# RMSNorm and QKV projection on one core: whole row tiles stored at once, crossbar transposes in fours, and a new order of the head

## The chip, the cores and the metric

One core of one Trainium2 chip. The metric is the device time in microseconds of one execution. The profile is of one execution, taken by the hardware profiler.

## What is computed

`x` has shape (8, 1024, 768), `w_qkv` (768, 2304), all float32. The rows of `x` are normalized and multiplied by the matrix:

```python
rms = np.sqrt(np.mean(x ** 2, axis=-1, keepdims=True) + eps)
x_norm = x / rms * gamma
return np.matmul(x_norm, w_qkv).astype(np.float32)
```

Flattened, that is 8192 rows by 768, times 768 by 2304: 25.2 MB read, 7.1 MB of matrix, 75.5 MB written.

## The kernel before

**Tiles.** The rows make 64 row tiles of 128. The contraction of 768 makes six blocks `ko` of 128. Row tiles 0 to 3 are done **directly**: `mm` multiplies one block by 512 (or 256) columns of the bf16 matrix `w_b`, and `evac` scales the sum out of PSUM. All others go in **pairs** p = 2 to 31 (row tiles 2p and 2p + 1) by a Strassen-like scheme with seven products in place of eight, for each of three column chunks c of 768 columns. A product (`product`, L686) is three matmuls of 384 columns. `osum` makes the four sums s1 to s4 of a pair's blocks, `quad` and `tsum` the eight matrix blocks of a chunk. `hold` copies a partial result out of PSUM, `join` (VectorE) adds it to another, and `last` (ScalarE) writes the fourth quarter.

**Path of a row tile.** `load_x` (SP queue) brings 384 KB; `pstat` (ScalarE, L634) sums the squares, `prms` and `precip` make the factor, `pcast` (VectorE, L648) writes the scaled tile in f16. Then it is transposed: `pxbar` (L652) by a crossbar DMA from SP, or `ptr` and `pcp` (L671, L456 and L458) by six PE transposes and a copy. Before, row tiles 4, 5, 7 and 9 take the second way, the other 56 of the pairs the first. The first four tiles are cast to bf16 without the factor (`cast`), transposed by PE (`tr`, L480) and copied (`cp`); their statistics are `stat`.

**The matrix.** `load_w` brings it in 16 pieces, `conv(piece, ko, engine)` multiplies by gamma and writes `w_b`. `bound`, `fold`, `bound_tr`, `bound_top`, `bound_all` and `scales` find the f16 scale of a chunk.

**Output buffers.** A buffer of the pool `outp` holds 1024 columns of one row tile (12 buffers; four small ones of `outs` for columns 2048 on). `w_b` is free after the head, and pieces of it serve as output buffers too (`spare`, `lent`). `store` and `pstore` (L740) write a chunk of 768 or 1024 columns from SP as soon as it is whole: 384 KB in rows of 3072 B, mostly.

**Order.** Each engine works through its instructions in the order in which the program issues them, and that order is written out: `at(time, fn, ...)` puts a step into a list that is sorted by the time key. The keys of the head (`PLAN`, pairs 2 to 14) are literals and set an order; they are no measured times. From pair `STEADY` = 15 on a loop makes them, with z the key at which chunk c of pair p begins, one `SLOT` = 0.4875 us per product and 21 slots per pair:

```python
                    when((-96, -103)[odd] + 7 * i, load_x, t)
                    when((-64, -71)[odd] + 7 * i, pstat, t)
                    when((-41.2, -53.8)[odd] + 4.1 * i, pcast, t)
                    when((-38.2, -50.8)[odd] + 4.1 * i, pxbar, t)
```

SP's queue holds all loads of x and of the matrix, all crossbar transposes and nearly all stores, in one order.

**The start of the head.** SP loads x tiles 1, 0, 2, then matrix pieces 4, 1, 2, 3, x tile 3, pieces 0, 6, 7, 5. PE transposes gamma, runs 14 warming matmuls on zeros (`idle`, L555), then transposes tiles 1, 0 and 2, and begins the direct matmuls (L516). ScalarE runs cast, stat, three copies, two stats, and then conv(0, 0) (L450).

Of the kernel before, what the change touches and what calls it, by code (L numbers as in the profile page):

```python
# [15 lines left out]
HEAD_END = 166.25  # L16
# [3 lines left out]
    (0.000, "load_x", 1), (1.160, "load_x", 0), (1.580, "load_x", 2), (5.030, "cast", 0, "DVE"), (5.031, "load_w", 4),  # L20
    (5.032, "load_w", 1), (6.820, "cast", 2, "DVE"), (6.821, "cast", 1, "ACT"), (6.822, "stat", 0),
    (6.823, "load_w", 2), (6.824, "load_w", 3), (6.825, "gamma_in"), (6.826, "idle", 14, 512), (6.827, "tr", 1),
    (7.480, "conv", 4, 5, "DVE"), (7.481, "tr", 0), (7.482, "cp", 0, "ACT"), (7.483, "tr", 2),
    (7.484, "cp", 1, "ACT"), (8.050, "mm", 0, 0, "5"), (8.141, "conv", 1, 2, "DVE"), (8.266, "mm", 1, 0, "5"),
    (8.267, "load_x", 3), (8.801, "conv", 2, 3, "DVE"), (8.802, "cp", 2, "ACT"), (8.803, "mm", 0, 0, "2"),
    (8.926, "mm", 1, 0, "2"), (9.142, "mm", 2, 0, "5"), (9.371, "mm", 2, 0, "3"), (9.372, "stat", 1),
    (9.461, "conv", 3, 4, "DVE"), (9.587, "mm", 0, 0, "3"), (9.803, "mm", 1, 0, "3"), (10.031, "mm", 0, 0, "4"),
    (10.032, "recip", 0), (10.451, "stat", 3), (10.452, "load_w", 0), (11.772, "conv", 0, 1, "POOL"),
    (11.773, "mm", 2, 0, "4"), (11.774, "conv", 0, 0, "ACT"), (11.775, "cast", 3, "DVE"), (11.776, "mm", 1, 0, "4"),
    (11.777, "tr", 3), (12.612, "mm", 1, 0, "01"), (13.043, "mm", 0, 0, "01"), (13.044, "load_w", 6),  # L30
    (13.045, "load_w", 7), (13.046, "stat", 2), (13.047, "load_w", 5), (13.092, "conv", 6, 2, "POOL"),
    (13.093, "load_w", 10), (13.094, "cp", 3, "DVE"), (13.095, "bound", 0, 1, "DVE"), (13.831, "conv", 6, 3, "DVE"),
    (13.971, "bound", 0, 0, "ACT"), (14.261, "recip", 2), (14.262, "mm", 2, 0, "012"), (14.263, "mm", 3, 0, "012345"),
    (14.264, "load_w", 8), (14.361, "recip", 1), (15.571, "evac", 2, 0, "ACT"), (15.572, "recip", 3),
    (15.573, "load_w", 9), (17.054, "conv", 10, 5, "POOL"), (17.055, "mm", 0, 512, "23"),
    (17.056, "mm", 2, 512, "23"), (17.057, "conv", 7, 4, "DVE"), (17.058, "conv", 7, 5, "DVE"),
    (17.059, "mm", 1, 512, "45"), (17.060, "mm", 0, 512, "54"), (17.145, "mm", 3, 512, "45"),
    (17.146, "conv", 5, 1, "DVE"), (17.147, "evac", 3, 0, "ACT"), (17.576, "mm", 2, 512, "45"),
    (17.577, "load_w", 15), (17.578, "evac", 1, 0, "ACT"), (17.579, "conv", 5, 0, "DVE"),
    (18.008, "mm", 1, 512, "23"), (18.009, "bound", 1, 0, "ACT"), (18.010, "load_x", 5),  # L40
    (18.011, "bound", 0, 2, "DVE"), (18.554, "fold", 0), (18.555, "mm", 1, 512, "01"), (18.871, "bound_tr", 0),
    (18.872, "conv", 10, 4, "POOL"), (18.873, "evac", 0, 0, "DVE"), (18.971, "conv", 8, 0, "ACT"),
    (19.364, "bound_top", 0), (19.365, "load_x", 4), (19.366, "conv", 8, 1, "POOL"), (19.367, "mm", 3, 512, "01"),
    (19.695, "conv", 9, 3, "POOL"), (19.724, "bound_all", 0), (19.844, "mm", 2, 512, "01"), (20.044, "scales", 0),
    (20.045, "load_w", 14), (20.275, "mm", 1, 1024, "01"), (20.707, "mm", 3, 1024, "45"),
    (20.708, "evac", 1, 512, "ACT"), (21.139, "mm", 2, 1024, "01"), (21.140, "conv", 9, 2, "POOL"),
    (21.141, "evac", 2, 512, "ACT"), (21.142, "load_x", 7), (21.570, "mm", 0, 512, "01"),
    (22.002, "mm", 0, 1024, "23"), (22.003, "bound", 1, 2, "DVE"), (22.434, "mm", 3, 512, "23"),
    (22.435, "load_x", 6), (22.866, "mm", 2, 1024, "45"), (23.297, "mm", 3, 1024, "01"),
    (23.298, "quad", 0, "b22", "ACT"), (23.299, "quad", 0, "b12", "POOL"), (23.300, "bound", 1, 1, "DVE"),  # L50
    (23.301, "pstat", 5), (23.729, "mm", 3, 1024, "23"), (24.035, "fold", 1), (24.036, "pstat", 4),
    (24.037, "conv", 15, 3, "POOL"), (24.215, "conv", 15, 5, "ACT"), (24.216, "evac", 3, 512, "DVE"),
    (24.217, "mm", 0, 1024, "01"), (24.645, "prms", 2), (24.646, "bound_tr", 1), (24.845, "evac", 3, 1024, "DVE"),
    (24.846, "mm", 0, 1024, "45"), (24.895, "conv", 15, 4, "ACT"), (24.896, "load_w", 13), (24.897, "load_w", 12),
    (25.144, "mm", 1, 1024, "23"), (25.145, "quad", 0, "b11", "POOL"), (25.146, "load_w", 11),
    (25.325, "evac", 0, 512, "ACT"), (25.925, "evac", 0, 1024, "ACT"), (25.926, "mm", 0, 2048, "345"),
    (25.927, "mm", 1, 2048, "345"), (25.928, "bound_top", 1), (26.231, "bound_all", 1), (26.351, "mm", 1, 1024, "45"),
    (26.352, "conv", 14, 1, "POOL"), (26.353, "precip", 2), (26.354, "pcast", 5), (26.705, "conv", 14, 2, "DVE"),
    (26.965, "pcast", 4), (26.966, "pstat", 6), (26.967, "mm", 2, 1024, "23"), (26.968, "load_x", 15),
    (27.515, "tsum", 0, "t1", "DVE"), (27.516, "evac", 1, 1024, "ACT"), (27.517, "ptr", 5),  # L60
    (28.095, "conv", 13, 4, "ACT"), (28.215, "pcp", 5, "DVE"), (28.216, "conv", 14, 0, "POOL"),
    (28.217, "mm", 3, 2048, "345"), (28.218, "mm", 0, 2048, "012"), (28.735, "conv", 13, 5, "ACT"),
    (28.855, "osum", 2, "s1", "DVE"), (28.856, "mm", 3, 2048, "012"), (28.857, "mm", 2, 2048, "345"),
    (28.884, "ptr", 4), (29.244, "mm", 1, 2048, "012"), (29.572, "mm", 2, 2048, "012"),
    (29.573, "evac", 3, 2048, "DVE"), (29.574, "load_x", 12), (29.575, "pstat", 7),
    (29.818, "store", 3, 2, 2048, 256), (29.819, "scales", 1), (30.238, "load_x", 8), (30.239, "pcp", 4, "DVE"),
    (30.240, "quad", 0, "b21", "POOL"), (30.345, "evac", 0, 2048, "ACT"), (30.498, "evac", 1, 2048, "DVE"),
    (30.898, "evac", 2, 2048, "DVE"), (30.899, "mm", 1, 1536, "45"), (30.900, "conv", 12, 3, "POOL"),
    (31.038, "store", 1, 2, 2048, 256), (31.039, "conv", 12, 2, "POOL"), (31.040, "conv", 11, 0, "POOL"),
    (31.041, "quad", 1, "b21", "POOL"), (31.042, "mm", 3, 1536, "45"), (31.043, "mm", 3, 1536, "23"),  # L70
    (31.458, "store", 2, 2, 2048, 256), (31.459, "mm", 2, 1536, "23"), (31.460, "bound", 2, 1, "DVE"),
    (31.461, "conv", 11, 1, "ACT"), (31.462, "quad", 1, "b11", "ACT"), (31.626, "mm", 3, 1536, "01"),
    (32.575, "prms", 3), (32.576, "product", 2, 0, 1), (32.978, "evac", 2, 1024, "DVE"), (32.979, "product", 2, 0, 2),
    (33.033, "mm", 2, 1536, "45"), (33.034, "hold", 2, 0, "a", "p1", "ACT"), (33.638, "precip", 3),
    (33.639, "store", 0, 2, 2048, 256), (33.738, "join", 2, 0, 0, 0, "b", "p1"), (34.288, "pcast", 6),
    (34.289, "load_x", 17), (34.290, "load_x", 16), (34.291, "load_x", 11), (34.998, "osum", 2, "s2", "DVE"),
    (34.999, "mm", 0, 1536, "23"), (35.000, "mm", 1, 1536, "01"), (35.001, "mm", 2, 1536, "01"),
    (35.002, "bound", 2, 2, "ACT"), (35.003, "mm", 0, 1536, "01"), (35.191, "mm", 1, 1536, "23"),
    (35.192, "bound", 2, 0, "ACT"), (35.193, "quad", 1, "b22", "POOL"), (35.623, "product", 2, 0, 5),
    (35.624, "tsum", 0, "t2", "DVE"), (36.110, "mm", 0, 1536, "45"), (36.111, "pcast", 7),  # L80
    (36.568, "osum", 2, "s4", "DVE"), (36.569, "product", 2, 1, 1), (36.570, "pxbar", 6),
    (36.888, "osum", 2, "s3", "DVE"), (36.889, "evac", 1, 1536, "ACT"), (37.029, "product", 2, 1, 2),
    (37.030, "load_x", 23), (37.125, "hold", 2, 0, "c", "p5", "ACT"), (37.126, "quad", 1, "b12", "POOL"),
    (37.208, "tsum", 1, "t1", "DVE"), (37.517, "product", 2, 0, 6), (37.908, "tsum", 1, "t3", "DVE"),
# [275 lines left out]
CW = 384  # L360
# [8 lines left out]
def kernel(  # L369
# [8 lines left out]
    nc = tc.nc  # L378
    f32 = mybir.dt.float32
# [15 lines left out]
    MT = M // P  # L395
    NT = 512
    inv_k = 1.0 / float(K)
    PARTS = [(0, 1024), (1024, 1024), (2048, N - 2048)]

    singles = ctx.enter_context(tc.tile_pool(name="singles", bufs=1))  # L400
    wst = ctx.enter_context(tc.tile_pool(name="wst", bufs=12))
# [436 lines left out]
```

## Time and profile before

| | us |
|---|---|
| median of three runs | 354.19 (353.32 to 355.4) |
| the profiled execution, its own time | 353.78 |
| its span | 352.0 |
| PE busy | 341.8 |
| VectorE / ScalarE / POOL busy | 265.3 / 242.1 / 118.0 |
| first unbroken run of direct matmuls begins | 14.52 |
| PE ends; last work of the chain ends | 348.0; 348.9 |
| DMA moved | 119.19 MB, 339 GB/s in the mean |

The page gives busy time, share of the span and the count of instructions of each engine; the span in 40 slices of 8.8 us with the busy share in tenths; DMA queues; the chain of work that ended last; groups of instructions by source line; and DMA issues with the median time from issue to landing. PE busy 97% says little by itself: where PE has idle time, and what ended that, is read from busy time by stretches and from the chain. In a line of the stretches come the window, its length, then for PE, PE's weight loads, VectorE, ScalarE and POOL the busy time and the count, then PE's granted clock, the DMA share and GB/s.

### The profile page before, as it was taken

What the parts mean: (1) busy time and instruction counts of PE and PEld (TensorE: products, weight loads), DVE (VectorE), ACT (ScalarE), POOL (GpSimd) and SP (SyncE); (2) the same over time, 40 slices, a digit from 0 to 9 for tenths busy, and PEclk for the clock granted to TensorE, in tenths of its full rate; (3) what the DMA queues carried; (4) which work ended last, traced back from release to release, by engine and by line L of the source; (5) the groups of instructions that cost most, each with busy time, mean ns of one, the idle gap of its engine ahead of it and who ended that gap; (6) DMA issues with size and microseconds to landing.
All of it is one profiled execution on the core that took longest, in us unless ns stands there. A gap on an engine that the chain in (4) does not pass through costs nothing.

```text
span 352.0 us, 6558 instructions
## 1 busy us (share of the span) xinstructions
PE 341.8 (97%) x2079; PEld 201.4 (57%) x2082; DVE 265.3 (75%) x504; ACT 242.1 (69%) x497; POOL 118.0 (34%) x130
## 2 busy tenths in 40 slices
PE   6799999999999999999999999999999999999995
PEld 2346555666666666656666565656666666666663
DVE  2689989888788987786776859677686867767663
ACT  4999988966776756757758575766757677564543
POOL 0187237413123105244404444251614444163000
PEclk9999999999999999999999999999999999999999
DMA  7998999999999999999999999999999999998565
GB/s 267 391 383 295 311 405 309 331 313 374 314 301 374 338 411 340 371 384 314 359 374 316 404 341 365 346 386 354 356 344 326 369 327 373 314 380 301 202 260 223
DMA packets 86238, 119.19 MB, mean 339 GB/s; under 512 B 49206, under 2 KB 51132, under 8 KB 86204
## 3 DMA queue, kind: packets, MB, share of 16 engines
q1 hardware_dynamic: 86048, 118.68, 100.8%
q8 instruction: 16, 0.26, 0.3%
q14 instruction: 18, 0.15, 0.1%
q10 hardware_dynamic: 156, 0.10, 0.1%
HBM read 32.25 MB, written 75.50 MB: 306 GB/s over the span
## 4 chain that ended last, share of the span: by engine, by line
PE 92%; ACT 4%; DVE 1%; issue 1%; DMA 1%; DVEq 0%; ACTq 0%
PE pm L686 85%; PE pm L516 5%; PE pm L555 2%; ACT sq L576 1%; ACT xT L458 1%; DVE ot L711 1%; DMA g<-in_gamma_dram 1%; ACT ot L534 0%; ACT sq L467 0%; ACT pp L695 0%; PE pm L671 0%; DVE xb L648 0%; ACT w_b L450 0%; PE pm L480 0%; DVE pp L693 0%
## 5 line engine op out<-in xcount | busy, mean ns | idle before, releaser
L686 PE MATMUL pm<-wq,su 128*128 128x384 f16 x1080 | 203.8, 326 | 0.3 <-DVE pp L693 0.3
L695 ACT ACTIVATE pp<-pm,sc 128x384 f32<-128x384 f32 x207 | 116.5, 581 | 75.0 <-PE pm L686 72.7
L686 PE MATMUL pm<-wq,xT 128*128 128x384 f16 x807 | 159.3, 326 | 1.0 <-DVE ot L711 0.6
L686 PEld LDWEIGHTS <-su 128*128 128x128 f16 x1080 | 105.5, 98 | 70.1 <-issue 0.5
L711 DVE SCALAR_TENSOR_TENSOR ot<-pm,sc,pp 128x384 f32<-128x384 f32 x172 | 100.3, 611 | 23.6 <-PE pm L686 21.4
L686 PEld LDWEIGHTS <-xT 128*128 128x128 f16 x807 | 78.7, 98 | 54.1 <-issue 1.1
L666 POOL TENSOR_TENSOR su<-xT 128x384 f16<-128x384 f16 x52 | 49.6, 956 | 154.3 <-DMA xT<-xb 82.5
L711 DVE SCALAR_TENSOR_TENSOR w_b<-pm,sc,pp 128x384 f32<-128x384 f32 x98 | 58.1, 613 | 28.5 <-PE pm L686 24.5
L693 DVE TENSOR_SCALAR pp<-pm,sc 128x384 f32<-128x384 f32 x63 | 38.4, 614 | 19.1 <-PE pm L686 18.8
L634 ACT ACTIVATE sq<-x_t 128x768 bf16<-128x768 f32 x60 | 50.1, 835 | 2.1 <-DMA x_t<-in_x_dram 2.0
L648 DVE TENSOR_SCALAR xb<-x_t,rstd 128x768 f16<-128x768 f32 x60 | 41.0, 688 | 0.5
L715 ACT ACTIVATE ot<-pm,sc 128x384 f32<-128x384 f32 x48 | 27.5, 576 | 11.7 <-PE pm L686 11.7
L715 ACT ACTIVATE w_b<-pm,sc 128x384 f32<-128x384 f32 x41 | 23.4, 576 | 9.3 <-PE pm L686 9.3
L666 POOL TENSOR_TENSOR su<-su,xT 128x384 f16<-128x384 f16 x24 | 22.7, 948 | 19.6 <-DVE su L666 9.5
L516 PE MATMUL pm<-w_b,xT 128*128 128x512 bf16 (+1 forms) x117 | 25.1, 358 | 1.9 <-ACT w_b L450 0.9
L666 POOL TENSOR_TENSOR su<-xT,su 128x384 f16<-128x384 f16 x24 | 22.4, 933 | 8.7 <-DVE su L666 7.0
L516 PEld LDWEIGHTS <-xT 128*128 128x128 bf16 x120 | 11.2, 98 | 12.5 <-ACT xT L458 1.7
L452 POOL TENSOR_SCALAR w_b<-wq,g_sb 128x512 bf16<-128x512 f32 (+1 forms) x13 | 8.5, 665 | 18.0 <-DMA wq<-in_w_qkv_dram 18.0
L634 ACT ACTIVATION_READ_ACCUMULATOR sq<-x_t 128x1 f32 x60 | 11.5, 192 | 0.0
L618 POOL TENSOR_SCALAR wq<-w_b,inv 128x1152 f16<-128x1152 bf16 x8 | 10.1, 1266 | 3.2 <-issue 2.6
L638 ACT ACTIVATE rms<-ssq,eps_sb 128x2 f32<-128x2 f32 x30 | 8.8, 293 | 0.0
L573 DVE TENSOR_REDUCE bnd<-w_b 128x1 f32<-128x1536 bf16 x5 | 8.6, 1742 | 0.1
(57 smaller groups left out, 94.9 us busy)
## 6 DMA issues: line engine op xcount, KB each, us to landing
out_dram<-ot SPq DMA_DIRECT2D x110, 384.0 KB, 4.8
out_dram<-w_b SPq DMA_DIRECT2D x68, 384.0 KB, 5.0
x_t<-in_x_dram SPq DMA_DIRECT2D x64, 384.0 KB, 5.5
wq<-in_w_qkv_dram SPq DMA_DIRECT2D x10, 512.0 KB, 9.1
out_dram<-ot SPq DMA_DIRECT2D x8, 512.0 KB, 7.4
wq<-in_w_qkv_dram SPq DMA_DIRECT2D x4, 256.0 KB, 6.0
xT<-xb SPq DMA_TRANSPOSE x56, 5.0
wq<-in_w_qkv_dram SPq DMA_DIRECT2D x2, 384.0 KB, 9.5
```

What stands on the lines that cost most here:

```text
L516: nc.tensor.matmul(out=PM[t, n0][:, :nl], lhsT=XT[t][:, ko, :], rhs=w_b[:, ko, n0:n0 + nl], start=(b == 1), stop=(b == KO))
L573: nc.vector.tensor_reduce(out=o, in_=v, axis=mybir.AxisListType.XY, op=amax, apply_absolute_value=True)
L618: nc.gpsimd.tensor_scalar(out=o, in0=quad_view(c, q), scalar1=INV[c], scalar2=1.0, op0=mult, op1=mult)
L634: nc.scalar.activation(out=sq, in_=X[t], func=AF.Square, accum_out=SS[p][:, t % 2:t % 2 + 1])
L638: nc.scalar.activation(out=r, in_=SS[p], func=AF.Sqrt, scale=inv_k, bias=eps_sb)
L648: nc.vector.tensor_scalar(out=XB[t], in0=X[t], scalar1=SS[t // 2][:, t % 2:t % 2 + 1], scalar2=None, op0=mult)
L666: (nc.vector if eng == "DVE" else nc.gpsimd).tensor_tensor(out=block(p, q), in0=block(p, x), in1=block(p, y), op=op)
L686: nc.tensor.matmul(out=PB[k][:, :CW], lhsT=block(p, a)[:, ko, :], rhs=WQ[c, b][:, ko, :], start=(first and ko == 0), stop=(ko == KO // 2 - ...
L693: nc.vector.tensor_scalar(out=o, in0=pb, scalar1=SC[c], scalar2=None, op0=mult)
L695: nc.scalar.activation(out=o, in_=pb, func=AF.Copy, scale=SC[c], bias=0.0)
L711: nc.vector.scalar_tensor_tensor(out=result(p, c, i, j), in0=PB[p, c, bank][:, :CW], scalar=SC[c], in1=PART[p, c, held], op0=mult, op1=add)
L715: nc.scalar.activation(out=result(p, c, 1, 0), in_=PB[p, c, "a"][:, :CW], func=AF.Copy, scale=SC[c], bias=0.0)
```

## The change

**Output buffers** hold a whole row tile: `outp` has 5 buffers of 2304 columns, `outs` is gone, and three rows fit into `w_b` (row tiles t >= 8 with t % 8 in 1, 4, 6). A row tile is stored once, by `rstore`, when all its chunks are done: 1.18 MB in rows of 9216 B. Only the last pair is stored in parts. Where SP had about 195 stores it has 70.

**The steady loop** issues the four loads of two pairs in a row, the four transposes of two pairs in a row, and moves statistics and casts ahead by 21 slots, one pair. `xin` goes from 9 to 10 buffers, `xbp` from 4 to 6.

**The head** has a new order throughout. Row tiles 7 and 9 are transposed by the crossbar, not by PE; 6 warming matmuls are left of 14; SP loads x tiles 2 and 1, piece 4, tile 0, pieces 2 and 3, tile 3, pieces 0, 1, 6, 7, 5, 8, 10, 9; PE transposes tiles 2 and 1 ahead of the warming matmuls. Between the direct matmuls and pair 6 the key order on SP is: transposes of 6 and 7, load 12, store of row 3, load 10, row 2, load 14, row 0, transposes of 8 and 9, row 1, load 16, transposes of 11 and 10, load 15, row 4.

The diff, of `PLAN` only the first keys:

```diff
-HEAD_END = 166.25
+HEAD_END = 164.31
 STEADY = 15
 PLAN = [
-    (0.000, "load_x", 1), (1.160, "load_x", 0), (1.580, "load_x", 2), (5.030, "cast", 0, "DVE"), (5.031, "load_w", 4),
-    (5.032, "load_w", 1), (6.820, "cast", 2, "DVE"), (6.821, "cast", 1, "ACT"), (6.822, "stat", 0),
-    (6.823, "load_w", 2), (6.824, "load_w", 3), (6.825, "gamma_in"), (6.826, "idle", 14, 512), (6.827, "tr", 1),
...
+    (2.400, "gamma_in"), (2.401, "load_x", 2), (4.040, "stat", 2), (4.041, "load_x", 1), (5.240, "stat", 1),
+    (5.241, "load_w", 4), (5.242, "cast", 2, "DVE"), (5.243, "cast", 1, "DVE"), (5.244, "load_x", 0),
+    (5.245, "tr", 2), (5.670, "tr", 1), (6.030, "idle", 6, 512), (6.031, "load_w", 2), (6.490, "conv", 4, 5, "POOL"),
...
-    xin = ctx.enter_context(tc.tile_pool(name="xin", bufs=9))
+    xin = ctx.enter_context(tc.tile_pool(name="xin", bufs=10))
-    xbp = ctx.enter_context(tc.tile_pool(name="xbp", bufs=4))
+    xbp = ctx.enter_context(tc.tile_pool(name="xbp", bufs=6))
-    outp = ctx.enter_context(tc.tile_pool(name="outp", bufs=12))
-    outs = ctx.enter_context(tc.tile_pool(name="outs", bufs=4))
+    outp = ctx.enter_context(tc.tile_pool(name="outp", bufs=5))
...
+    spare = [N * i for i in range(KO // 2)]
+    lent = {}
+
+    def row(t):
+        if t not in OUT:
+            if t >= 8 and t % 8 in (1, 4, 6):
+                s = lent[t] = spare.pop(0)
+                OUT[t] = w_b.rearrange("p k n -> p (k n)").bitcast(f32)[:, s:s + N]
+            else:
+                OUT[t] = outp.tile([P, N], f32, name="ot")
+        return OUT[t]
...
+    def rstore(t):
+        nc.sync.dma_start(out=of[t * P:(t + 1) * P, :], in_=OUT[t])
+        if t in lent:
+            spare.append(lent.pop(t))
...
-                    when((-96, -103)[odd] + 7 * i, load_x, t)
-                    when((-64, -71)[odd] + 7 * i, pstat, t)
-                    when((-41.2, -53.8)[odd] + 4.1 * i, pcast, t)
-                    when((-38.2, -50.8)[odd] + 4.1 * i, pxbar, t)
-                when((-54.5, -61.5)[odd], prms, p)
-                when((-42, -54.6)[odd], precip, p)
+                    when((-96, -116.8)[odd] + 0.1 * i, load_x, t)
+                    when((-85, -92)[odd] + 7 * i, pstat, t)
+                    when((-62.2, -74.8)[odd] + 4.1 * i, pcast, t)
+                    when((-33.2, -54)[odd] + 0.1 * i, pxbar, t)
+                when((-75.5, -82.5)[odd], prms, p)
+                when((-63, -75.6)[odd], precip, p)
...
-                when(8.0, pstore, p, c, 0)
+                if final:
+                    when(8.0, pstore, p, c, 0)
+                elif c == N_CH - 1:
+                    when(8.0, rstore, 2 * p)
...
-                when(15.6, pstore, p, c, 1)
+                if final:
+                    when(15.6, pstore, p, c, 1)
+                elif c == N_CH - 1:
+                    when(15.6, rstore, 2 * p + 1)
```

## The prediction

> **What bounds the kernel now.** I read the busy line of the page first, then busy time by stretches, then the chain that ended last.
>
> ```profile
> PE 341.8 (97%) x2079; PEld 201.4 (57%) x2082; DVE 265.3 (75%) x504; ACT 242.1 (69%) x497; POOL 118.0 (34%) x130
> DMA  7998999999999999999999999999999999998565
> q1 hardware_dynamic: 86048, 118.68, 100.8%
> xT<-xb SPq DMA_TRANSPOSE x56, 5.0
> ```
>
> Two resources look full, TensorE and the 16 DMA engines. The stretches say which one sets the end.
>
> ```profile
> 8.48:14.50 6.02, 4.27 (x36) 2.37 (x35) 2.93 (x7) 5.09 (x11) 1.38 (x2) 1.00 1.04 394
> 30.00:42.00 12.00, 11.57 (x76) 6.78 (x76) 11.70 (x25) 11.23 (x20) 5.71 (x7) 1.00 0.89 261
> 220.00:260.00 40.00, 40.00 (x248) 24.06 (x246) 29.40 (x56) 27.45 (x59) 15.06 (x16) 1.00 1.07 361
> ```
>
> The first time after the stretch is its length, the next the PE time. From 220 us on PE never stops: 248 matmuls in 40 us, 163 ns each for 384 columns. DMA is full as well, but nobody on PE waits for it. So from there the change can only lose. From 14.5 us PE lacks some 0.4 us at 30 to 42, and 0.27, 0.22 and 0.42 us at 150, 195 and 217. The rest that can be won lies ahead of 14.52 us, in this chain (start, length, what):
>
> ```profile
> 3.06 5.58 PE pm L555 x14
> 8.64 0.69 PE pm L480 x12
> 9.35 2.20 ACT xT L458 x3
> 11.55 0.84 ACT sq L467 x2
> 12.71 0.83 ACT sq L467 x2
> 13.77 0.71 ACT w_b L450
> 14.52 0.59 PE pm L516 x2
> ```
>
> The 14 warming matmuls hold PE to 8.64, though VectorE and ScalarE had cast both first x tiles by 5.42. The transposes start late, so ACT's three copies do, so its statistics do, and the conversion conv(0,0) behind them ends at 14.5. PE waits 0.9 us for it. By 14.52 it has done 11 of 120 direct matmuls.
>
> **What the Trainium skill says.** *TensorE: Matmul & The Clock Gate*, Part 1: an idle array runs at half rate until about 3.4 us of sustained work. The trace agrees: warming matmuls start 0.425 us apart until 8.04 and direct ones 0.216 us apart later. It also says that ACT and DVE are strict first-in-first-out, so one late operand holds all that is queued behind it. *DMA: Bandwidth & Descriptors*, Anatomy of one DMA: a fixed 2.0 us plus bytes/436e3 (fitted on GpSimd's path). For a 1.18 MB row tile that makes an estimate of 4.7 us. The trace has no such transfer; its nearest row is the 384 KB store, 2.5 us near the end where DMA is free (the formula: 2.9) and 4.8 overall.
>
> **The change, part by part.** The sum is made against the profiled execution: 353.78 us, of which 352.0 is span. The median of the three runs is 354.19, 0.41 above it.
>
> *(1) Six warming matmuls instead of 14, behind two tiles' transposes: -1.1 us.* In the trace x tiles land at 3.87 and 4.86, and from the third on the conversions that wait for DMA (9.18 us at 1.97 MB queued, 12.36 at 3.15, 13.62 at 3.67) lie on a line of 0.38 MB per us. The new order queues x2, x1, w4, x0, w2, w3, x3, w0, w1, w6. So w0 (2.88 MB) lands at 11.6 instead of 12.4, and w1 (3.15 MB) at 12.3. Transposes of tiles 2 and 1 end by 6.1 on a cold array, the six matmuls at 8.7. Nine direct matmuls and two tiles' transposes follow; wholly cold they take 9 x 0.427 + 12 x 0.107 = 5.1 us, warm half of it; with the clock released near 10.5 they end by 12.3. The conversion of w1 on POOL (0.69) ends at 13.0, and 11 direct matmuls are done: where before stood at 14.52. That is 1.5 earlier. Against it, running closer to the loads costs about 0.25 (conv(6,2) now sits behind a stat and a bound on ACT, ready at 16.0, wanted at 15.76) and 0.2 (w10, landing at 19.1). Bounds: -1.9 (no feeding stall) and +0.5 (clock released a window later, and the loads lag 1 us).
>
> *(2) Tiles 7 and 9 go to the crossbar: -0.7 us, then +1.0.* Twelve PE transposes at 0.34 us for six are 0.68 us of PE time, all on the path, and the copies of 0.56 (DVE) and 0.81 (ACT) go. What replaces them is two DMAs on SP, 1.2 to 2.6 us to issue and 2.6 to 7.0 to land. Tile 9's comes behind tile 8's, some 6 us after its cast; VectorE's osum(4,s1) stands 3.7 us of work behind that cast and waits 1 to 2 us, with all joins behind it. The whole-row store of tile 1 is moved behind these two transposes on SP, and row 8 takes its buffer: VectorE's first join into it comes 6 to 7 us after the cast of 9, the store lands after 6 to 9. Both waits overlap; part is absorbed by PE's 8 PSUM banks. I take +1.0; bounds 0 and +2.5.
>
> *(3) The rest of the head: -0.3.* Three small gaps (0.27, 0.22, 0.42) had VectorE behind. The order there is new, so I take half of them as gone (-0.45), and +0.15 for ACT waiting on tile 15, whose load stands some 5.2 us ahead of its statistic (loads in steady state: 5.0 to 6.1). Bounds -0.9 and +1.5.
>
> *(4) 1.18 MB stores in place of 0.39 MB ones: 0.* About 190 stores become 70. SP's issue time is no bound: in two pairs' 20.5 us it issues 4 transposes (1.9 each, the median from 240 us on) and 8 copies (0.6), 12 us. The bytes stay, PE never reads a store. If this cover goes, it costs through buffers: 8 row buffers at 2 rows per 10.25 us are 41 us round, used for 8 us plus a landing of 5 to 8; some 25 us spare. Bounds 0 and +0.5.
>
> *(5) Transposes four in a row, casts and statistics one pair earlier: 0.* pstat, prms, precip and pcast all move by 21 slots, a whole pair, so ACT's and VectorE's order inside a pair is unchanged. Transposes still have 13 us to their first use against 5.0. With fewer changes between copies and transposes (one group in 20.5 us, not three; the rate falls to 134 GB/s at 243 us, behind such a group) DMA gains 1 to 2 us per two pairs, which nobody waits for.
>
> *(6) Loads four in a row, but 11 slots (5.4 us) ahead of the first statistic, not 32: 0, with a tail.* They are issued right behind the second row's store. Copies land one per 0.92 us when the queue is full, and 2.5 us after issue when it is empty: 1.6 + 2.75 for the row, + 0.92, gives 5.3 us after the store's issue. ACT wants the tile 6.0 us after it, and has about 0.3 us of slack. So 0 is likeliest; upper bound in the second rival.
>
> The tail (349 to 352) keeps its stores. Sum: -1.1 - 0.7 + 1.0 - 0.3 = -1.1, about 352.7 against 353.78, and **353.1** against the median.
>
> **The rivals.** *The head's gain stays whole.* If the landings of (2) come at 4 us and the small gaps go, it is -1.5 - 0.7 - 0.4 - 0.9 = -3.5 at most, 350.7 against the median. For it: VectorE lags only because PE did; PE idled 0.9 us just ahead of 14.52. Against it: from 20 to 60 us VectorE is 87 to 97% busy, and its work up to the cast of tile 8 is the same.
>
> *ACT starves in every second pair: slower.* The load behind the row's store lands late, ACT's pstat waits, the holds behind it wait, and PE cannot go on into a bank not read:
>
> ```profile
> 263.80 0.58 ACT L695 ACTIVATE pp<-pm,sc 128x384 f32<-128x384 f32 x1 [0.88 <-PE pm L686]
> 264.28 0.83 ACT L634 ACTIVATE sq<-x_t 128x768 bf16<-128x768 f32 x1
> 265.10 0.57 ACT L715 ACTIVATE ot<-pm,sc 128x384 f32<-128x384 f32 x1
> 265.57 0.58 ACT L695 ACTIVATE pp<-pm,sc 128x384 f32<-128x384 f32 x1
> ```
>
> The last of these must be read before a product 0.3 us later. If 1 us of transposes or of the earlier row's store is still queued when the row's store is issued, the tile lands 6.3 us or more after it, and anything past 6.3 is lost on PE, eight times (even pairs 16 to 30). At 0.5 us each that is 4 us: 357. It decides from 6.3 us. For it: DMA is full before. Against it: loads landed within 6.1 us of their own issue, behind as many bytes.
>
> *The store does what it says and nothing comes of it,* head included (the start's gain is eaten at pairs 4 and 5): 353.5 to 354.5. For it: the loads end the first waits in both orders.
>
> **How the numbers follow.** What can be told from no change here is 0.5%, 1.8 us. Small net gain or none (the sum and the last rival), from 352 to 355: 0.53, of it 0.13 below 352.4. Whole gain, 350.8 to 352.4: 0.22. Slower by ACT or by VectorE's waits, 355 to 359: 0.25. Faster is 0.13 + 0.22 = 0.35, same 0.40, slower 0.25. The range leaves out the lowest 5% and the highest 10%: 350.9 to 357.3.
>
> **What would show it.** Right: the first unbroken run of direct matmuls starts near 13.0, PE 100% busy from 220, PE matmul count down by 20, waits "DVE su <- DMA xT" and "DVE ot <- DMA out" of about 1 us near 55, transpose landings in one group. Wrong: "ACT sq L617 <- DMA x_t" or the like over 2 us in total, PE below 39.9 in 220 to 260, a start later than 14, or a product stream that is no earlier at 60 us.

## The result, and the profile after

The changed kernel takes **371.92 us** (median of four, 370.22 to 372.34) against 353.75 in the same comparison: a ratio of 1.0496, 95% interval 1.0447 to 1.0544. That is 18.2 us slower, where the prediction said 353.1 and at most 357.3. The profiled execution has a span of 370.2 us. Where one execution of a kernel lay over 1.5% above its fastest (one in all, 386.25 us in experiment 6), it is left out of the figures.

The busy line, the granted clock by slices, the queue and the loads of the page after (last number of an issue line: median us from issue to landing):

```profile
PE 344.5 (93%) x2059; PEld 201.8 (54%) x2062; DVE 273.1 (74%) x506; ACT 241.1 (65%) x495; POOL 121.5 (33%) x129
PEclk9999989999999989999999899999999999999999
q1 hardware_dynamic: 69792, 119.06, 95.1%
x_t<-in_x_dram SPq DMA_DIRECT2D x64, 384.0 KB, 6.9
```

PE does nearly the same number of matmuls (20 fewer, as foretold) in 18 us more. Bytes are nearly unchanged (119.06 MB on SP's queue against 118.68), and the queue is no fuller than before (95.1% against 100.8%). But loads of x land after 6.9 us in the median (5.5 before), and the clock row has three 8s, at 46 to 56, 130 to 139 and 204 to 213 us, where the row of the kernel before has only 9s.

Busy time by stretches, of after and, for the three with the largest loss, of before:

```profile
8.48:14.50 6.02, 4.97 (x32) 2.45 (x31) 4.06 (x13) 5.18 (x10) 0.69 (x1) 1.00 1.04 393
30.00:42.00 12.00, 11.72 (x69) 6.12 (x68) 10.93 (x20) 11.39 (x21) 7.38 (x8) 1.00 0.90 284
42.00:50.00 8.00, 5.88 (x28) 2.80 (x26) 7.44 (x13) 4.34 (x9) 4.35 (x3) 0.79 1.02 426
128.00:140.00 12.00, 8.63 (x44) 4.65 (x43) 5.56 (x11) 4.58 (x11) 4.25 (x5) 0.86 1.07 272
196.00:212.00 16.00, 11.50 (x62) 6.40 (x61) 7.78 (x15) 7.02 (x14) 2.18 (x3) 0.90 1.00 378
220.00:260.00 40.00, 39.47 (x243) 23.56 (x241) 30.78 (x54) 26.32 (x57) 15.60 (x15) 1.00 0.97 343
```

```profile
42.00:50.00 8.00, 8.00 (x50) 4.54 (x49) 6.42 (x16) 6.57 (x15) 4.51 (x4) 1.00 1.03 412
128.00:140.00 12.00, 12.00 (x76) 7.21 (x75) 9.23 (x18) 7.03 (x16) 4.42 (x5) 1.00 1.08 358
196.00:212.00 16.00, 15.78 (x98) 9.41 (x97) 11.04 (x21) 10.43 (x24) 5.13 (x6) 1.00 1.07 356
```

In stretches three to five of after PE does 28, 44 and 62 matmuls; before did 50, 76 and 98 there. At 0.163 us each the missing 22, 32 and 36 are 3.6, 5.2 and 5.9 us: 14.7 of the 18.2. The rest is smaller stops between 140 and 180 and a steady loss from 220 on (243 matmuls instead of 248 in 40 us). So the loss is not spread evenly: it sits in a few stops, and then a trickle.

What ends those stops (waits of after: who, for whom; total us, times, longest):

```profile
ACT sq L617 <- DMA x_t<-in_x_dram: 12.9, 5, 4.9
PE pm L669 <- ACT pp L678: 9.3, 4, 4.5
PE pm L669 <- DVE btop L573: 2.1, 1, 2.1
```

The first stop, at 42, ends on VectorE (the last line; see experiment 4). In the later ones ScalarE's pstat waits for its x tile, and PE waits for ScalarE's hold behind it. Three long waits of ScalarE, ended at 131.63, 157.51 and 206.68, are 12.1 of the 12.9 us. From 220 to 340 us it waits for x tiles only 0.2 us in all. The longest one, first on ScalarE and then on PE, from the timeline of after:

```profile
206.68 0.84 ACT L617 ACTIVATE sq<-x_t 128x768 bf16<-128x768 f32 x1 [4.88 <-DMA x_t<-in_x_dram]
207.43 0.19 ACT L617 ACTIVATION_READ_ACCUMULATOR sq<-x_t 128x1 f32 x1
207.53 0.56 ACT L689 ACTIVATE w_b<-pm,sc 128x384 f32<-128x384 f32 x1
207.99 0.57 ACT L678 ACTIVATE pp<-pm,sc 128x384 f32<-128x384 f32 x1
```

```profile
208.61 1.77 PE L669 MATMUL pm<-wq,su 128*128 128x384 f16 x6 [4.50 <-ACT pp L678]
210.18 2.12 PE L669 MATMUL pm<-wq,xT 128*128 128x384 f16 x6
```

After 4.50 us of idleness PE takes 1.77 and 2.12 us for six matmuls; six at 201.50, ahead of the stop, took 1.14. The granted clock in that time:

```profile
209.00:210.00 1.00, 1.00 (x5) 0.48 (x4) 0.21 (x1) 0.54 (x2) 0.00 (x0) 0.50 1.09 446
```

So the stop costs its length and some more, because PE starts again at half the clock (0.50): 5.9 us by the missing matmuls, for a wait of 4.50.

And why the load is late, in SP's queue of after around the burst at 140 us:

```profile
136.57 0.53 SPq L521 DMA_DIRECT2D out_dram<-ot  x1
137.19 1.49 SPq L521 DMA_DIRECT2D out_dram<-w_b  x1
138.74 1.18 SPq L521 DMA_DIRECT2D out_dram<-ot  x1
142.40 0.33 SPq L521 DMA_DIRECT2D out_dram<-w_b  x1
142.87 2.42 SPq L521 DMA_DIRECT2D out_dram<-ot  x2
145.34 5.15 SPq L418 DMA_DIRECT2D x_t<-in_x_dram  x4
```

Six row stores, 7.1 MB, are issued within 9 us (called the burst below), and the four loads right behind them. The tile view gives the loads' landings, the times from issue until the tile is there:

```profile
DMA to landing us min/median/max: 11.5/11.8/12.1
```

The plan has 5.4 us between the first of such four loads and its statistic; this distance is called the lead. The first two of the four are an odd pair's (in the loop `odd` is `(p + 1) % 2`, so the first number of `(-96, -116.8)[odd]` is for pairs 15, 17 to 31). The even pair's two have 24.8 slots, 12.1 us. The chain of waits runs through three loads of this kind:

```profile
123.03 8.59 DMA x_t<-in_x_dram
...
145.34 12.15 DMA x_t<-in_x_dram
...
196.36 10.30 DMA x_t<-in_x_dram
```

### The profile page after: what moved, and what is told of

The parts are those of the page before. It is cut to its first block, busy times and chain, and to the rows that moved or that the text cites. A ratio compares the mean times of both kernels' runs of the same rounds, so it can differ in the third digit from the quotient of the medians.

```text
span 370.2 us, 6171 instructions
## 1 busy us (share of the span) xinstructions
PE 344.5 (93%) x2059; PEld 201.8 (54%) x2062; DVE 273.1 (74%) x506; ACT 241.1 (65%) x495; POOL 121.5 (33%) x129
## 3 DMA queue, kind: packets, MB, share of 16 engines
q1 hardware_dynamic: 69792, 119.06, 95.1%
## 4 chain that ended last, share of the span: by engine, by line
PE 68%; DMA 18%; DVE 6%; issue 4%; ACT 2%; SPq 2%; DVEq 0%; ACTq 0%
PE pm L669 68%; DMA x_t<-in_x_dram 14%; DMA out_dram<-ot 2%; DMA wq<-in_w_qkv_dram 2%; DVE ot L685 1%; DVE xb L631 1%; DVE wq L607 1%; DVE w_b L685 1%; ACT pp L678 1%; SPq L521 1%; DVE pp L676 1%; SPq L418 0%; ACT sq L617 0%; SPq L423 0%; DVE su L649 0%
## 5 line engine op out<-in xcount | busy, mean ns | idle before, releaser
L669 PE MATMUL pm<-wq,su 128*128 128x384 f16 x1080 | 205.9, 329 | 9.3 <-ACT pp L678 9.3
L669 PE MATMUL pm<-wq,xT 128*128 128x384 f16 x807 | 161.2, 330 | 5.5 <-DVE btop L573 2.1
L685 DVE SCALAR_TENSOR_TENSOR ot<-pm,sc,pp 128x384 f32<-128x384 f32 x165 | 97.5, 612 | 48.4 <-PE pm L669 37.9
L649 POOL TENSOR_TENSOR su<-xT 128x384 f16<-128x384 f16 x49 | 48.1, 990 | 156.6 <-PE pm L669 92.8
L685 DVE SCALAR_TENSOR_TENSOR w_b<-pm,sc,pp 128x384 f32<-128x384 f32 x105 | 62.5, 611 | 15.8 <-PE pm L669 13.4
L617 ACT ACTIVATE sq<-x_t 128x768 bf16<-128x768 f32 x60 | 50.3, 838 | 13.2 <-DMA x_t<-in_x_dram 12.9
L689 ACT ACTIVATE ot<-pm,sc 128x384 f32<-128x384 f32 x68 | 38.8, 577 | 19.5 <-PE pm L669 19.4
L631 DVE TENSOR_SCALAR xb<-x_t,rstd 128x768 f16<-128x768 f32 x60 | 45.6, 765 | 0.4
L649 POOL TENSOR_TENSOR su<-su,xT 128x384 f16<-128x384 f16 x24 | 23.2, 966 | 28.6 <-PE pm L669 22.6
L649 POOL TENSOR_TENSOR su<-xT,su 128x384 f16<-128x384 f16 x27 | 26.6, 987 | 16.7 <-DVE su L649 8.6
L689 ACT ACTIVATE w_b<-pm,sc 128x384 f32<-128x384 f32 x21 | 12.1, 577 | 4.9 <-PE pm L669 4.8
L617 ACT ACTIVATION_READ_ACCUMULATOR sq<-x_t 128x1 f32 x60 | 11.6, 194 | 0.0
L431 ACT ACTIVATE w_b<-wq,g_sb 128x512 bf16<-128x512 f32 (+1 forms) x12 | 7.6, 644 | 2.2 <-DMA wq<-in_w_qkv_dram 2.1
```

The lines of the kernel that those rows point to most:

```text
L617: nc.scalar.activation(out=sq, in_=X[t], func=AF.Square, accum_out=SS[p][:, t % 2:t % 2 + 1])
L631: nc.vector.tensor_scalar(out=XB[t], in0=X[t], scalar1=SS[t // 2][:, t % 2:t % 2 + 1], scalar2=None, op0=mult)
L649: (nc.vector if eng == "DVE" else nc.gpsimd).tensor_tensor(out=block(p, q), in0=block(p, x), in1=block(p, y), op=op)
L669: nc.tensor.matmul(out=PB[k][:, :CW], lhsT=block(p, a)[:, ko, :], rhs=WQ[c, b][:, ko, :], start=(first and ko == 0), stop=(ko == KO // 2 - ...
L685: nc.vector.scalar_tensor_tensor(out=result(p, c, i, j), in0=PB[p, c, bank][:, :CW], scalar=SC[c], in1=PART[p, c, held], op0=mult, op1=add)
L689: nc.scalar.activation(out=result(p, c, 1, 0), in_=PB[p, c, "a"][:, :CW], func=AF.Copy, scale=SC[c], bias=0.0)
```

## The experiments

Names beginning with a_ are built on the kernel after, those with b_ on the kernel before. Ratios are against before, run beside each; in brackets the ratio and its 95% interval.

**1. Only the odd pairs' loads earlier: a part comes back.**

```diff
-                    when((-96, -116.8)[odd] + 0.1 * i, load_x, t)
+                    when((-117, -116.8)[odd] + 0.1 * i, load_x, t)
```

> The kernel after, and in its steady loop the two loads of an even pair 21 slots (10.2 us) earlier, so that loads go two and two instead of four in a row, each at least 25 slots ahead of its statistic. Theory 1 (the loads are too close to the statistics; ScalarE waits, PE stops and cools): the lost PE time at 128-140, 140-180 and 196-212 us (5.2, 3.1 and 6.2 us by the count of matmuls) goes nearly whole, the stop at 42-50 and the 2 us lost between 225 and 308 stay: 357 to 360. Theory 2 (the blocks on SP's queue, four transposes in a row behind 1.18 MB stores, delay whatever comes behind them; the loads are only the first to show it): the loads are still behind the same blocks, only a part comes back: 363 to 370.

By the code the pairs that this line moves are the odd ones, those with the lead of 5.4 us, and not the even ones.

Measured 363.68 us (1.0262, 1.022 to 1.0304): 8.2 us better than after, and at the lower end of theory 2's range. The stop at 128 to 140 is gone. Others came at 140 to 160, where VectorE waited for a row buffer whose store took 8.35 us to land, and at 220 to 260. The new place interleaves the loads with the transposes. The even pairs' loads, 12.1 us ahead, landed after 16.2 us at the burst (issued at 140.25) and after 11.4 us at 217.62.

**2. Only the transposes apart again: nothing.**

```diff
-                    when((-33.2, -54)[odd] + 0.1 * i, pxbar, t)
+                    when((-38.2, -50.8)[odd] + 4.1 * i, pxbar, t)
```

> The kernel after, and in its steady loop the transposes apart as in the kernel before (one every 4.1 slots, two groups per two pairs) instead of four in a row. Theory 1 (load lead): the loads keep their lead, and those at 123 us stand behind transposes of the head that are not moved, so 128-140 stays and the later stops get smaller only in part: 365 to 371. Theory 2 (blocks on SP's queue): SP is held 2 to 3 us at a time and not 7 to 10, the loads of the loop land within 7 us, the stops at 140-212 (9.3 us) go: 360 to 364.

Measured 370.9 (1.0469, 1.0411 to 1.0526). ScalarE waits 13.8 us for x tiles, not less. The 1.0 us to after is not clear of the noise. A block on SP made by the row of transposes is not the cause by itself.

**3. The loop's old slots under the new stores and the new head.** All six `when` lines of loads, statistics, factors, casts and transposes as before; `rstore`, buffers and `PLAN` as after.

> The kernel after with its whole-row buffers, row stores and head, but loads, statistics, casts and transposes of the steady loop at the slots of the kernel before. Theories 1 and 2 (timing of the loop): all stops from 128 us on go, the one at 42-50 stays: 355 to 358. Theory 3 (the 1.18 MB stores themselves burden the DMA queues or the buffers): the stores are all there, so 364 to 371.

Measured 357.12 (1.0082, 1.0059 to 1.0105). So 14.8 of the 18.2 us are the loop's slots, and 3.0 are the head and the row stores. What its tile view says of the same burst of stores (loads issued 139.4 to 148.9):

```profile
DMA to landing us min/median/max: 11.9/16.0/16.2
```

These loads are **slower** than those of after, and hardly anyone waits: 0.6 us of ScalarE in the whole run, because they have 15.6 us and more. The burst is there in both. But six lines changed, so this run alone doesn't tell the lead from the places of transposes, statistics and casts.

By count of matmuls the 3.0 us arise in two places. Up to 128 us PE did 706 against 735, up to 220 us 1254 against 1292; 20 of each difference are the warming matmuls and PE transposes left out by the change. So 9 are behind at 128 and 18 at 220, 1.5 and 2.9 us.

**4. One step of the head off POOL.** In the profile after, VectorE's osum at 41.52 takes 2.52 us and not 0.34, and ends as POOL's tsum does:

```profile
40.94 2.88 POOL L607 TENSOR_TENSOR wq<-wq 128x1152 f16<-128x1152 f16 x1
```

```profile
41.52 2.52 DVE L649 TENSOR_TENSOR su<-xT 128x384 f16<-128x384 f16 x1
```

```diff
-(45.841, "tsum", 1, "t4", "POOL")
+(45.841, "tsum", 1, "t4", "DVE")
```

> The kernel after with one step of the head, tsum(1, t4), on VectorE instead of POOL. In the profile VectorE's osum at 41.52 us takes 2.52 us instead of 0.34, until POOL's tsum (40.94 to 43.82) ends, and PE stops at 42.84. Theory A (VectorE was held off by POOL's instruction): the stop at 42-50 us (28 matmuls instead of 50, 3.6 us) gets smaller by 2 to 3.6 us: 368.3 to 370. Theory B (the stop has another cause, PE would wait for VectorE's queue anyway, which gets 0.74 us longer): 371 to 372.5.

Measured 372.49 (1.0502, 1.0453 to 1.0552): no gain, the time of theory B. Yet the same osum now took 0.35 us, and the stretch 42 to 50 did 44 matmuls instead of 28. VectorE had been held off beside POOL, as theory A says. Of the 16 matmuls gained, 2.6 us, 9 were left at 128 us, and at 220 the run was 3 behind after; ScalarE waited 15.6 us for x tiles in place of 12.9. A head that is ahead then waits longer for the next late tile.

**5. The old slots, but transposes in a row.**

```diff
-                    when((-38.2, -50.8)[odd] + 4.1 * i, pxbar, t)
+                    when((-27.5, -48.3)[odd] + 0.1 * i, pxbar, t)
```

> The kernel after with its row stores and head and the loop's slots of the kernel before (that was 357.1), but the four transposes of two pairs in a row (slots -27.5 and -48.3). Loads keep 32 slots of lead. Theory 1 (short lead of the loads): transposes in a row cost nothing by themselves, 356 to 358. Theory 2 (SP held by four transposes in a row behind 1.18 MB stores is a cause of its own, which is why only 8 of the 15 us came back with earlier loads): 360 to 366.

Measured 372.66 (1.0525, 1.0493 to 1.0557), worse than either theory said. Here the four transposes stand behind stores and loads, and SP's queue shows what that costs:

```profile
249.53 14.53 SPq L635 DMA_TRANSPOSE xT<-xb  x4
```

In after they stand behind two row stores only, and four take 6.5 us (276.12 to 282.65). A cycle of this kernel takes 23.2 us of SP (249.53 to 272.71) where PE needs 20.5. The edit also cut the transposes' lead to 10 us, against landings of 12.6 in the median from 225 to 300 us. So a row of transposes with that lead does harm, if it stands behind a backlog. Which of the two it is, the shorter lead or the row, this run doesn't tell.

**6. The old slots, but the loads late.**

```diff
-                    when((-96, -103)[odd] + 7 * i, load_x, t)
+                    when((-75, -95.8)[odd] + 0.1 * i, load_x, t)
```

> The same base (357.1), transposes apart, but the four loads in a row with the lead of the kernel after: 11 slots to the first statistic (slots -75 and -95.8). Theory 1: ScalarE waits for x tiles some 10 us in total and the stops come back: 364 to 371. Theory 2 (the short lead hurts only behind a row of transposes): 356 to 360.

Measured 379.64 (1.0714, 1.0667 to 1.0761): against number 3 the short lead of the loads, set in a row, costs 22.5 us, with transposes apart. That is worse than the whole change.

```profile
ACT sq L617 <- DMA x_t<-in_x_dram: 20.4, 8, 4.9
PE pm L669 <- ACT pp L678: 16.5, 8, 4.5
```

Eight waits for x tiles, eight stops of PE. From 120 to 330 us the loads landed after 5.4 to 8.3 us, 7.0 in the median; in after from 220 to 310 it was 5.7 to 6.9. These loads stand between two groups of transposes. That a lag in every cycle makes it worse than after fits this, but is not shown apart.

**7. The same line in the kernel before**, with its 384 KB stores.

> The kernel before with nothing changed but the loads of its loop: four in a row, 11 slots ahead of the first statistic instead of 32. Stores stay 384 KB, transposes apart. Theory 1 (lead alone): 362 to 370. Theory 3 (a late load also needs the 1.18 MB stores ahead of it in the queue): within 1 us of before's 354.2, up to 357.

Measured 363.75 (1.0259, 1.0222 to 1.0297): 9.6 us from one line, without any 1.18 MB store. ScalarE's waits in the whole run, and the landings of the loads from 120 to 330 us, where the lead was 5.4:

```profile
ACT sq L634 <- DMA x_t<-in_x_dram: 14.3, 9, 3.8
DMA to landing us min/median/max: 4.1/5.8/7.2
```

**8. Number 4 on the base of number 3.**

> The base of 357.1 us with tsum(1, t4) on VectorE instead of POOL. In the kernel after this step won 16 of the 22 matmuls lost at 42-50 us and gave all of it back at the later stops for x tiles. If those stops were the reason, they are gone here and the gain stays: 354 to 355. If the stop at 42-50 is slack of another kind (VectorE's 0.74 us more, later waits), 356.5 to 357.5.

Measured 356.67 (1.0069, 1.0041 to 1.0096): 0.4 us better, which is within the noise, and not 2 to 3. The stretch 42 to 50 has 43 matmuls instead of 28, but the chain of waits now runs through row buffers not yet stored, the first two of them new against number 3:

```profile
38.22 6.18 DMA out_dram<-ot
...
66.62 6.87 DMA out_dram<-ot
...
133.27 9.49 DMA out_dram<-w_b
```

A row buffer is free only after its last chunk and a landing of 6.2 to 9.5 us here. That this is what took the gain is read from the chain and not tested.

**9. Thirds from row buffers.** In the loop of after, `pstore` after each chunk in place of `rstore` after the third.

> The kernel after, but in its steady loop each row is stored in three parts of 384 KB, each as soon as its chunk is done, from the same whole-row buffers. Loads and transposes keep their slots. Theory 1 or 2 (lead of the loads, transposes in a row): it stays slow, 364 to 373. Theory 3 (1.18 MB stores issued together make the backlog that the loads stand behind): the stops from 128 us on go, 357 to 361.

Measured 378.62 (1.0688, 1.065 to 1.0725): 6.7 us slower than after. So the size of the loop's stores is not what makes it slow; large ones were a relief to it. The burst at 140 us is made of stores of the head and stays as it was.

**10. DMA alone,** the traffic of two pairs per cycle in five orders.

> DMA traffic alone, all on SP's queue, nothing computed (rows stored are zeros, the last part of each cycle is what is varied): per cycle the traffic of two pairs, 4 loads of 384 KB, 4 row stores of 1.18 MB, 4 transposes. Five orders: (1) copies, then four transposes in a row; (2) transposes two and two; (3) one transpose after each row and load; (4) no transposes; (5) as (1) with stores of 384 KB. The kernel after has 20.5 us per cycle. Theory 2 (a row of transposes does not overlap copies: 14.4 us of copies at 437 GB/s plus 6.5 us of transposes): (1) and (5) take 20.5 to 23 us, (4) 14 to 15.5, (2) and (3) less than (1) by 2 us or more. Rival (the grouping does not matter to DMA, only the place in the queue does): (1), (2), (3) within 1 us of each other.

Stretches of this kernel (length, then at the end the DMA share and GB/s; each one cycle, the third a mean over copies only; a single execution):

```profile
23.17:43.37 20.20, 0.00 (x0) 0.00 (x0) 1.00 1.04 351
89.49:107.63 18.14, 0.00 (x0) 0.00 (x0) 1.00 1.07 372
200.00:230.00 30.00, 0.00 (x0) 0.00 (x0) 1.00 1.03 421
276.30:296.94 20.64, 0.00 (x0) 0.00 (x0) 1.00 1.03 332
```

Four in a row: 20.2 us in each of three cycles. Two and two: 18.1, the next cycle 19.0. One after each row and load: 19.6 to 20.0. Without transposes 6.29 MB at 421 GB/s are 14.9. Thirds and four in a row: 20.6 and 21.6. Theory 2 had two and two about right and one at a time wrong. PE's cycle is 20.5 us. So the order of after leaves 0.3 us per cycle to make good a delay, thirds leave nothing, and two and two leave 1.5 to 2.4. The own order of the kernel before, with 384 KB stores and transposes apart, is not among the five. The DMA share is above 1.00 in all of them and tells none of this.

**11. Half the transposes away, the lead as in after.**

```diff
-                    when((-33.2, -54)[odd] + 0.1 * i, pxbar, t)
+                    when((-33.2, -54)[odd] + 0.1 * i, share if i else pxbar, t)
```

> The kernel after, but in its steady loop the odd row tile of each pair is not transposed: it uses the transposed tile of the even one (half of the rows hold wrong values from row tile 31 on). Everything else keeps its slot, the lead of the loads too; per two pairs two transposes, some 3.3 us of DMA, are gone. Capacity of DMA: with 3.6 us of slack in a cycle the lateness is made good, the stops from 140 us on go; the one at 128-140 can stay: 356 to 363. Lead alone: the loads still stand behind the rows' stores, 366 to 372.

Measured 367.31 (1.0373, 1.0345 to 1.0401), 4.6 us better than after, within the range of lead alone. ScalarE still waits 11.4 us for x tiles. Capacity is a part, not the whole.

**12. Loads from ScalarE's queue** (`nc.scalar.dma_start` in the loop).

> The kernel after with the loads of its steady loop issued from ScalarE's queue instead of SP's, at the same slots. SP's order (a load is issued only when SP is through with its transposes and stores): loads are issued on time and land within 7 us, the stops from 128 us on go at least by half: 357 to 364. Capacity of DMA or lead alone: the loads are issued earlier but share the same 16 engines with the rows' stores, landing 8 to 12 us: 366 to 375.

Measured 372.69 (1.053, 1.0497 to 1.0562). The loads landed no earlier, after 9.9 and 14.1 us in the first two groups and 8.5 us in the median of all. Yet ScalarE waited only 3.8 us for x tiles, not 12.9: in place of that it was held issuing four loads, 4.96 and 4.39 us in the first two groups, and PE waited behind it as before. So the run changes two things at once. It shows that another queue doesn't make the tiles land earlier; whether SP's order has a share in the loss it leaves open.

**13. How much lead?** In the kernel before, loads four in a row, the lead varied:

```diff
-                    when((-96, -103)[odd] + 7 * i, load_x, t)
+                    when((-96, -116.8)[odd] + 0.1 * i, load_x, t)      # b_row_loads
+                    when((-85.5, -106.3)[odd] + 0.1 * i, load_x, t)    # b_lead21
```

> The kernel before with the loads of its loop four in a row but 32 slots (15.6 us) or more ahead of the statistic. Lead alone: within 1 us of before, 353.5 to 355. Four in a row cost by themselves: 357 to 363.7.

> The same with 21.5 slots (10.5 us) ahead of the first statistic. If the lead has to cover the landing behind a backlog, and that is 5 to 8 us with 384 KB stores, it is enough: 353.5 to 356. If any shortening costs: near the middle of 354.1 and 363.8, 358 to 360.

Measured 354.38 (1.0021, 0.9997 to 1.0045) and 354.69 (1.0018, 1.0 to 1.0036). Four in a row cost nothing that can be told here. With 15.6 and 10.5 us of lead the time is that of before to 0.2%; with 5.4 it is 9.6 us more. Landings with 10.5 us, from 120 to 330 us:

```profile
DMA to landing us min/median/max: 5.3/6.6/8.5
```

The lead of 10.5 us is longer than the longest of these landings, the lead of 5.4 (number 7) shorter than the median of its own. Numbers 7 and 13 differ in this one line alone.

**14. And in the kernel after?** Loads behind the third row's store (9.2 us of lead), or ahead of the transposes (15.7 us):

```diff
-                    when((-96, -116.8)[odd] + 0.1 * i, load_x, t)
+                    when((-103.9, -124.7)[odd] + 0.1 * i, load_x, t)   # a_lead19
+                    when((-117.3, -138.1)[odd] + 0.1 * i, load_x, t)   # a_lead32
```

> The kernel after with its loads still four in a row, but right behind the third row's store of a cycle and not the fourth's: 19 slots (9.2 us) ahead of the first statistic instead of 11. Lead alone: the stops from 128 us on go by two thirds or more (landings of 12 us behind the burst at 140 still show), 358 to 363. If the row of transposes keeps it slow: 365 to 372.

> The kernel after with its loads ahead of the four transposes: 32 slots (15.7 us) of lead for the first statistic, but the transposes now stand behind two stores and four loads. Lead alone: all stops for x tiles go, the one at 42-50 stays: 356 to 359. If the row of transposes is late behind a backlog (12 to 15 us to land in the run with transposes in a row and long lead, against 13 us to first use here): 362 to 370.

Measured 367.15 (1.0363, 1.0333 to 1.0393) and 363.76 (1.0268, 1.0209 to 1.0326). Both lie in the range of the row of transposes. With 9.2 us the tiles behind the bursts are still late (landings up to 12.2 us). With 15.7 ScalarE waits for them only 0.6 us in all, and yet 6.6 us more are lost than in number 3. Waits of a_lead32:

```profile
DVE w_b L685 <- DMA out_dram<-w_b: 4.5, 1, 4.5
ACT sq L617 <- DMA x_t<-in_x_dram: 0.6, 1, 0.6
PE pm L669 <- DVE w_b L685: 5.3, 3, 4.0
```

What is late next is a row buffer: the store of an earlier row took 8.9 us, VectorE's join waited 4.5 for it, and PE did 89 matmuls from 140 to 160 us (122 before), 5.4 us. The chain of waits has a second late transfer, a transpose issued at 212.28 that took 7.00 us. By number 10 DMA has 0.3 us of slack per cycle with such a row of transposes. That whatever stands last in the queue is then late, x tiles in after, row buffers and a transpose here, fits all of this and is an inference.

**15. The first term of the prediction by itself,** in the kernel before:

```diff
-(6.826, "idle", 14, 512)
+(6.826, "idle", 6, 512)
```

> The kernel before with 6 warming matmuls instead of 14 and nothing else: the first term of the prediction by itself. If PE's late start is what delays the first direct matmuls, the unbroken run begins 0.5 to 1.2 us earlier than 14.52 us and the time is 0.3 to 1 us shorter. Rival: the loads of the matrix end the first waits in both, and the array is colder: within 0.3 us, or up to 0.5 us longer.

Measured **352.96** (0.9976, 0.9961 to 0.9991): 0.65 us faster than before beside it, clear of the noise though small. PE now waits for the load of matrix piece 0, from the chain of waits and the timeline:

```profile
4.64 8.41 DMA wq<-in_w_qkv_dram
```

```profile
13.91 6.42 PE L516 MATMUL pm<-w_b,xT 128*128 128x512 bf16 x28 [1.06 <-ACT w_b L450]
```

The unbroken run begins at 13.91 and not 14.52. Loading that piece earlier, ahead of x tile 3 (`load_x` 3 and its statistic and transposes moved behind):

> The kernel before with 6 warming matmuls (that was 353.0 against 353.6) and matrix piece 0 loaded ahead of x tile 3, tile 3's statistic and transposes behind the first use of piece 0. In the run with 6 warming matmuls PE waited 1.06 us for the conversion of piece 0, which waited for its load (issue 4.64, landing 13.05). If that load is the bound now, it lands 0.6 to 0.9 us earlier: 352.0 to 352.7. Rival: what is moved behind it (tile 3) is late instead: 352.8 to 353.6.

Measured 353.89 (0.9991, 0.9975 to 1.0006): what it brings is lost again. The first 15 direct matmuls then take 4.98 us, 0.33 each, where 11 took 2.73 with the 6 warming matmuls alone, 0.25 each. Whether the late tile 3 is the reason, as the rival says, is not shown.

## Why the prediction was wrong

**The step that failed is (6),** "Loads four in a row, but 11 slots (5.4 us) ahead of the first statistic, not 32: 0, with a tail". The mechanism was seen, and is the second rival: ScalarE starves, the holds behind pstat wait, PE cannot go on. Its terms were wrong in three places.
- *The landing.* The step counted 5.3 us from the store's issue to the tile, with one row store in the queue. In the steady part this came near: a store issued at 243.59, its tile there 6.2 us later, 0.07 us ahead of the statistic. At the stop of 206 us it was 10.7 (store issued 195.98, tile there at 206.66). The step has no term for the stretch between head and loop, where rows 8, 9 and 18 to 21 are stored together: six and five row stores stand ahead of the loads at 145 and 196 us, and two stores behind slow transposes ahead of those at 123. The argument against the rival, "loads landed within 6.1 us of their own issue, behind as many bytes", came from a queue fed with evenly spaced thirds, and from 240 to 300 us; over the whole loop of before, 120 to 296 us, they took up to 6.7, past the 6.3 from which the rival decides. Number 7 shows that even there 5.4 us would have been too short.
- *The price of a stop.* For "At 0.5 us each that is 4 us" came 9.3 us of PE in four waits, up to 4.5 each, and after two of them PE started again at half its clock (granted 0.50 from 134 to 137 and from 209 to 212 us). A small lateness in every cycle was priced; what came was large and in the transition. The rival also named the wrong pairs: the short lead is that of the odd pairs, nine of them from 15 to 31.
- *The chance.* 0.25 for slower, for a wait with 0.3 us of slack against a full queue, was too little. A margin cut from 15.6 to 5.4 us beside landings of 5.0 to 6.1 should have been the likeliest case.

**(5) was wrong in sign,** as far as number 10 goes. The step said that DMA gains 1 to 2 us per two pairs with fewer changes between copies and transposes. Number 10 measures a row of four as the slowest order with 1.18 MB stores: 1.2 to 2.1 us more than two and two, 0.2 to 0.6 more than one at a time, and 20.2 of PE's 20.5 us. Numbers 11 (4.6 us) and 14 (6.6 us still lost with the long lead) show that the transposes have a part in the loss. The trickle from 220 us on is not explained by the row alone: a_lead19, with the same row, did 248 matmuls from 220 to 260 as before did, though 289 against 298 from 260 to 308.

**(4), the stores: 0 was half right.** The estimate of 4.7 us for a 1.18 MB store met medians of 5.5 and 4.9 us (from `ot` and from `w_b`). The size costs DMA nothing, rather the reverse (numbers 9 and 10). But "8 row buffers, some 25 us spare" holds for evenly spaced rows only. Around the burst a buffer's store landed after 8.9 to 9.5 us (numbers 8 and 14). Once the x tiles were on time, PE waited 0.9 us behind it in number 8 and lost 5.4 us in number 14.

**(1) was right in mechanism,** and in the change itself larger than expected: at 14.5 us 20 direct matmuls are done where before had done 11, and the first unbroken run begins at 11.80, not near 13.0. By itself, without the new order of the loads, the shorter warming gave 0.65 us (number 15). PE was at full rate earlier than the 10.5 us of the step: seven direct matmuls from 8.92 on took 1.67 us, 0.24 each. Of the clock the prediction says that its trace agrees with "about 3.4 us of sustained work"; it agrees in the half rate, but the warming matmuls from 2.99 on kept to that rate until 8.04, 5.0 us.

**(2) and (3) gave the start away again.** At 40 us all direct matmuls are done in both kernels, and after is 8 products' matmuls ahead of before (26 against 18), 1.3 us; at 50 us it is 12 behind. Head and row stores together are +3.0 (number 3), where -1.1 was expected. The wait foreseen near 55 us ("DVE su <- DMA xT") did not come; the one that came, VectorE beside POOL's tsum at 41.5 us, 3.6 us of PE at 42 to 50 of which number 4 got 2.6 back for a time, was not on the list.

Three of the signs named for a wrong forecast are in the profile: 12.9 us of "ACT sq L617 <- DMA x_t", PE at 39.47 in 220 to 260, and a product stream that is no earlier at 60 us (121 matmuls of products against 131). The sign of a late start is not: the start was early.

**Shown and not shown.** Shown: on the base of before the lead decides by itself (5.4 against 10.5 us: 9 us), on the base of number 3 it does too (22.5 us); the loop's slots are 14.8 of the 18.2 us; smaller stores in the loop don't help. Shown as a part: the row of transposes. Not settled: how the 14.8 us divide between lead and transposes, since the two are not additive (8.2 come back with the loads moved ahead of the transposes, 1.0 with spread transposes, 14.8 with both and the old places of statistics and casts), and whether SP's order has a share.

## What to carry to other kernels

The lead of a prefetch (a load issued ahead of its use) has to cover the landing behind the worst backlog that its queue ever holds, not the median landing; look for it where two schedules meet, and where many large stores are issued together. In this case a DMA share of 100% did not tell whether there was slack: the traffic run alone in its order, its cycle compared with the compute's, did. When one wait is removed, ask what else stands in the same full queue: it may be late next.

## What the runs showed of the hardware

- The order of transposes among copies changes the time of the same bytes: 20.2 us with four in a row, 18.1 to 19.0 two and two, 19.6 to 20.0 one at a time (number 10).
- SP's time to issue four crossbar transposes is 6.5 us behind two row stores (after, 276.12) and 12.6 to 15.8 us behind four loads and four row stores (numbers 10 and 5); nothing else of SP's is issued meanwhile.
- Loads issued behind the burst of six 1.18 MB stores land after 11.5 to 16.2 us from SP's queue (after, numbers 1 and 3), and after 12.5 to 15.3 from ScalarE's (number 12).
- A VectorE f16 tensor_tensor took 2.52 us beside a POOL tensor_tensor, until 0.2 us after that one's end, and 0.35 us where that one was gone (number 4).
